# Background transfers of a Strassen stage: pinned in program order, handed out one at a time, with fewer steps

## The chip, the cores and the metric

The kernel runs on one core of a Trainium2 chip. The metric is the device time of one execution in microseconds; lower is better. The core has five engines with a queue each: PE (TensorE, the matrix engine), DVE (VectorE), ACT (ScalarE), POOL (GpSimd) and SP (SyncE, which only issues transfers). Each engine takes its queue in order. DMA transfers are issued from SP, ACT and POOL; only POOL's can add to what they write.

## The reference

One layer of a hybrid decoder trunk: the input (16 prepended meta tokens and 1024 tokens of 1024 channels) is normalised, projected, and read by three causal mixers: gated DeltaNet (`dn`, 8 heads), short gated convolution (`sc`) and Mamba-2 SSD (`sd`). Their outputs meet in a gated sum and an output projection:

```python
xn = rms_norm(x, norm_pre)
proj = xn @ w_in                      # every mixer's inputs, and the gate logits
ys = stack([y_ssd, y_sc, y_dn])
branch = einsum("btnw,nwd->btnd", ys, w_branch)
gates = sigmoid(gate_logits)          # (tokens, 3, 1024)
merged = sum(gates * branch, axis=2)
return x + rms_norm(merged @ w_out, norm_post)
```

All in float32, with seven 1024x1024x1024 products in the last part: three for the gates, three for the branches, one for the output.

## The kernel before

The kernel has two parts. The first (up to about 1325 us) projects the stream and runs the mixers: eight heads of `dn` (`dn_mix`), then eight tiles of `sd` (`sd_mix`). These are long chains of small operations on PE, DVE, ACT and POOL; `weave` fills PE between them with the dense projections of the next head or of `sc`. A mixer is a generator: at each `yield` the program takes some dense matmuls. The weights of a dense job are loaded by SP (L148), cast by ACT (L156) and their rest taken by DVE (L157), one job ahead.

The second part is the Strassen stage. Each of the seven products is a group of seven half-size products, 49 steps in all, and a step is four quarters (`q`) of 12 matmuls of 128x512: 48 matmuls. For each operand on the right (`x`, `dn`, `sc`, `sd`, `wo`) there are seven blocks of 1 MB in HBM: the quarters `11` and `22`, the negated `n21`, and the sums `t1` to `t4`. The program computes the sums by transfers alone: `sums` copies a block on POOL's queue and adds a second to it (an accumulating transfer), eight transfers for one operand:

```python
for dst, a, b in (("t1", "n12", "11"), ("t2", "t1", "22"),
                  ("t3", "n12", "22"), ("t4", "t2", "n21")):
    GP.dma_start(o[dst], o[a])
    GP.dma_start(o[dst], o[b], accum_op=ALU.add, max_dma_last_dim=2048)
```

During step n, `t_load` asks on SP for the two pieces (`tr`, 512 KB each) of step n+2; `t_prep` casts those of step n+1 (ACT `th`, DVE `tl`), `w_prep` its weights (ACT and DVE `w`), `left_sum` forms the sums on the left (DVE), `finish` takes the results off. Left blocks (`a11`, `a12`, `a21`, `a22`, 1 MB each; `a__...` in the trace) of the next group are loaded at steps 3 to 6 of a group, those of the first group at the stage's start. The first two steps take their right operand from the stream in SBUF (`xh`, `xl`).

Four kinds of background work make the operands. `right_x` (in head 0) stores the stream's quarters, the negated ones by way of ACT and a tile of the pool tag `t` (five buffers, shared with the mixers' rows and raw convolution inputs), the second half `xl` by accumulating transfers; then `sums("x")`. `right_wo` (in head 2) does it for `w_out`. `beside` takes one piece of such work at every third yield. `sc` stores its blocks on SP and starts `sums("sc")` after its last tile; `sums("dn")` runs beside `sd` tile 1. For `sd` the rows must be scaled by a norm that is known only after the last tile: `scale_tasks` (in steps 2 to 8 of the stage, one task at each quarter) loads a 1 MB block of `y_sd` as four pieces, multiplies it on DVE by the broadcast `rins`, stores it from ACT, and after four blocks starts `sums("sd")`.

Three things set the order. The program's text gives each instruction a rank. A scheduler then orders each engine's queue by simulated time: it takes the first in rank among those whose inputs it takes as landed, so that an instruction with nothing to wait for may come out far ahead of its place. And the chip takes each queue in that order, whatever lands when. `tc.keep_in_program_order` ties an instruction behind the one before it in the program on its engine.

Lines that the change and the steps of the prediction touch: `sums` L119 to L127, stores of `dn` L732, `sc` L765, `y_sd` L884, `rin_d` L904; `right_x` L906 (ACT L922, L924, POOL L913, L926); `right_wo` L930 (L936, L938, L941); `left blocks` L1047, `t_load` L1093, `t_prep` L1103 and L1104, `w_prep` L1112 to L1120, `left_sum` L1126, `out_setup` L1190 (`gpost`, asked for at step 42), `scale_tasks` L1221 to L1248 (`ys` L1234, L1239, L1243). In `dn_mix`, L636 is a memset on POOL that the delta solve needs at each level.

## Time and profile before

| | us |
|---|---|
| median of 3 runs (lowest, highest) | 1901.55 (1897.69, 1906.21) |
| profiled execution | 1900.59 |
| its span in the trace | 1898.3 |

| engine | busy us | share of the span |
|---|---|---|
| PE | 1824.3 | 96% |
| DVE | 1263.6 | 67% |
| ACT | 839.5 | 44% |
| POOL | 189.7 | 10% |

The trace moves 225.76 MB by DMA. The span is from the first to the last instruction that the profiler saw. PEclk is the clock that TensorE was granted, as a share of its full speed (1.00 is 2.4 GHz, 0.50 is 1.2 GHz). In the chain of waits each piece is what the next one waited for, followed back from the end. A wait for several things is put down to the one that came last. Transfers are named by what they write and read (`out<-in`), with the line and queue that issued them.

### The profile page before, as it was taken

The page shows a single profiled execution, that of the slowest core. Times are in us where ns is not written, and L with a number is a line of the kernel's source. Part 1 is how long each engine was busy: PE and PEld are TensorE (multiplying, and loading weights), DVE is VectorE, ACT ScalarE, POOL GpSimd, SP SyncE. Part 2 cuts the span into 40 slices and gives each one's busy share as a digit, 9 for nine tenths or more (in the row PEclk, how much of TensorE's full clock was granted, in tenths as well). Part 3 has the DMA queues.
Part 4 walks back from the last instruction along what each step waited for, and adds up shares of the span by engine and source line. Part 5 has one row for each costly group of instructions (what it writes and reads, how often), then busy time and mean ns, then how long its engine had stood idle before and what let it go on. Part 6 is the DMA issues. An engine that isn't in the chain of part 4 may idle for free.

```text
span 1898.3 us, 27585 instructions
## 1 busy us (share of the span) xinstructions
PE 1824.3 (96%) x11115; PEld 1578.8 (83%) x11115; DVE 1263.6 (67%) x1866; ACT 839.5 (44%) x1353; POOL 189.7 (10%) x335
## 2 busy tenths in 40 slices
PE   3998999999999999999999999999889999999997
PEld 3896989888998989888889899887668888888886
DVE  4554675656656656575756887786566857867687
ACT  4452534425243342434434556452335455455444
POOL 2021101101011110101001111110000000000000
PEclk8999999999999999999999999999889999999999
DMA  6568113821117221111123423221999443544532
GB/s 194 115 163 192 56 46 123 227 62 40 50 46 209 70 61 40 45 56 46 34 79 88 126 89 96 62 87 34 326 327 280 155 161 128 177 150 139 178 109 91
DMA packets 153258, 225.76 MB, mean 119 GB/s; under 512 B 11009, under 2 KB 97214, under 8 KB 152298
## 3 DMA queue, kind: packets, MB, share of 16 engines
q1 hardware_dynamic: 135162, 162.65, 27.1%
q0 software_dynamic: 12976, 46.66, 10.6%
q10 hardware_dynamic: 4992, 14.68, 2.0%
q8 instruction: 87, 1.43, 0.3%
q14 instruction: 41, 0.34, 0.1%
HBM read 192.41 MB, written 75.61 MB: 141 GB/s over the span
## 4 chain that ended last, share of the span: by engine, by line
PE 82%; DMA 7%; DVE 6%; issue 2%; ACT 1%; SPq 0%; POOL 0%; DVEq 0%; ACTq 0%; POOLq 0%
PE py L1141 5%; PE py L1140 5%; PE py L1139 5%; PE pz L1141 3%; PE pz L1140 3%; PE pz L1139 3%; DMA a__13462<-in_w_in_dram 1%; DMA ys<-y_sd 1%; DMA a__13776<-in_w_branch_dram 1%; DVE w L157 1%; DMA won<-in_w_out_dram 1%; DVE gt L1217 1%; DMA wo<-in_w_out_dram 1%; DMA xt<-in_x_dram 0%; DMA x_n<-xn 0%
## 5 line engine op out<-in xcount | busy, mean ns | idle before, releaser
L1141 PE MATMUL py<-th,w 128*128 128x512 f32 x432 | 170.1, 394 | 5.7 <-DVE w L1117 5.7
L1139 PE MATMUL py<-th,w 128*128 128x512 f32 x432 | 169.7, 393 | 1.7 <-ACT u L1151 1.7
L1140 PE MATMUL py<-tl,w 128*128 128x512 f32 x432 | 169.5, 392 | 1.9 <-DVE tl L1104 1.9
L1104 DVE TENSOR_TENSOR tl<-tr,th 128x1024 fp32r<-128x1024 f32 x94 | 114.1, 1222 | 67.4 <-ACT th L1103 66.8
L1103 ACT CAST th<-tr 128x1024 fp32r<-128x1024 f32 x94 | 98.4, 1052 | 106.0 <-PE py L1141 52.6
L1139 PE MATMUL pz<-th,w 128*128 128x512 f32 x320 | 124.5, 389 | 0.0
L1140 PE MATMUL pz<-tl,w 128*128 128x512 f32 x320 | 124.5, 389 | 0.0
L1141 PE MATMUL pz<-th,w 128*128 128x512 f32 x320 | 124.5, 389 | 0.0
L157 DVE TENSOR_TENSOR w<-raw,w 128x1024 fp32r<-128x1024 f32 x84 | 103.5, 1232 | 10.5 <-ACT w L156 9.8
L1141 PEld LDWEIGHTS py<-th,w 128*128 128x128 f32 x432 | 82.1, 190 | 23.5 <-DVE w L1117 6.5
L1140 PEld LDWEIGHTS py<-tl,w 128*128 128x128 f32 x432 | 82.0, 190 | 19.5 <-DVE tl L1104 2.3
L156 ACT CAST w<-raw 128x1024 fp32r<-128x1024 f32 x84 | 88.0, 1048 | 23.1 <-PE sc2h L180 4.0
L1139 PEld LDWEIGHTS py<-th,w 128*128 128x128 f32 x432 | 82.1, 190 | 19.2 <-ACT u L1151 2.1
L1140 PEld LDWEIGHTS pz<-tl,w 128*128 128x128 f32 x320 | 60.1, 188 | 12.5
L1139 PEld LDWEIGHTS pz<-th,w 128*128 128x128 f32 x320 | 60.1, 188 | 12.4
L1141 PEld LDWEIGHTS pz<-th,w 128*128 128x128 f32 x320 | 60.1, 188 | 12.4
L1151 ACT COPY u<-py 128x1024 f32<-128x1024 f32 x30 | 30.4, 1013 | 43.6 <-PE py L1141 38.3
L1164 DVE TENSOR_TENSOR u<-pz,u 128x1024 f32<-128x1024 f32 x30 | 36.6, 1219 | 7.6 <-PE pz L1141 7.6
L239 PE MATMUL xp<-ident,xg 128*128 128x128 f32 (+1 forms) x72 | 11.0, 304 | 21.2 <-DVE xg L233 20.8
L1170 ACT ACTIVATE gt<-u 128x1024 f32<-128x1024 f32 x14 | 14.8, 1061 | 31.7 <-DVE u L1164 31.5
L239 PEld LDWEIGHTS xp<-ident,xg 128*128 128x128 f32 (+1 forms) x72 | 9.4, 162 | 22.4 <-issue 20.9
L470 ACT ACT_TABLE_LOAD x18 | 23.1, 1283 | 4.5 <-PE sd3z L180 1.1
(1878 smaller groups left out, 5622.2 us busy)
## 6 DMA issues: line engine op xcount, KB each, us to landing
raw<-in_w_in_dram SPq DMA_DIRECT2D x84, 512.0 KB, 3.9
tr<-x_t SPq DMA_DIRECT2D x24, 512.0 KB, 4.1
tr<-x SPq DMA_DIRECT2D x10, 512.0 KB
ys<-y_sd SPq DMA_DIRECT2D x16, 256.0 KB, 10.2
tr<-dn_t SPq DMA_DIRECT2D x8, 512.0 KB, 6.0
tr<-sc_t SPq DMA_DIRECT2D x8, 512.0 KB, 3.7
tr<-sd_t SPq DMA_DIRECT2D x8, 512.0 KB, 3.5
tr<-wo_t SPq DMA_DIRECT2D x8, 512.0 KB, 3.6
```

The source lines that it names most:

```text
L156: A.copy(wh, raws[i])
L157: V.tensor_tensor(wl, raws[i], wh.bitcast(F32), ALU.subtract)
L239: PE.transpose(pv[:, k, :], xg[:n, kk * P:(kk + 1) * P], ident[:n, :n])
L470: lambda o, c0, n: A.activation(dst[:, c0 - META:c0 - META + n], o, fn), name=name)
L1103: A.copy(h, src)
L1104: V.tensor_tensor(l, src, h.bitcast(F32), SUB)
L1139: PE.matmul(o, lhsT=w[:, 0, k, cs], rhs=r1, start=fresh and k == 0, stop=False, skip_group_check=not fresh)
L1140: PE.matmul(o, lhsT=w[:, 0, k, cs], rhs=r2, start=False, stop=False, skip_group_check=not fresh)
L1141: PE.matmul(o, lhsT=w[:, 1, k, cs], rhs=r1, start=False, stop=k == HK - 1, skip_group_check=not fresh)
L1151: A.copy(t, g.ps["y", u])
L1164: V.tensor_tensor(k, t, k, ADD)
L1217: V.scalar_tensor_tensor(o, o, tot, fin["x", t][:, es], ALU.mult, ADD)
```

## The change

- Blocks `n12` are gone. `quarters` names for each quarter the blocks it is stored into: a negated upper right quarter goes straight into `t1` and `t3`, and `sums` adds `11` and `22` to them. `t2` and `t4` are made as before. Six transfers per operand are left.
- `background` pins a transfer in program order on its queue. `sums` and all transfers of `right_x` and `right_wo` use it.
- `right_x` adds or negates the pair `xh`, `xl` on DVE in one instruction per half quarter, and stores the result from ACT. The diagonal blocks of `w_out` are no longer copied: sums and the stage read them from `w_out` (`wo_straight`).
- `beside` takes a piece at every ninth yield and does not drain the rest; `early` (x, then w_out) runs beside all eight heads, `late` (sums of `dn`) beside the `sd` tiles.
- The stores of `sc`, `y_sd` and `rin_d` are issued by ACT instead of SP.
- `scale_tasks` works on eight pieces of 512 KB, with two buffers (tag `gpost`) and one row buffer of its own, one half piece per step from step 5 to 20 (`q` = 2).
- `sums("sc")` is taken at steps 3, 5, ... 13 and `sums("sd")` at steps 23, 25, ... 33, each piece behind a copy of one column (`tick`) on POOL that reads the step's `th`.

```diff
@@ -111,19 +111,25 @@
...
     OPS = ("11", "n21", "t2", "t3", "t1", "t4", "22")
-    opd = {s: {o: dram.tile([P, HK, HALF], F32, name=f"{s}_{o}") for o in OPS + ("n12",)}
+    opd = {s: {o: dram.tile([P, HK, HALF], F32, name=f"{s}_{o}") for o in OPS}
            for s in ("x", "dn", "sc", "sd", "wo")}
-    def quarter(s, i, j):
-        return opd[s][("" if i == j else "n") + f"{i + 1}{j + 1}"]
-    def sums(s):
-        o = opd[s]
-        for dst, a, b in (("t1", "n12", "11"), ("t2", "t1", "22"), ("t3", "n12", "22"), ("t4", "t2", "n21")):
-            GP.dma_start(o[dst], o[a])
-            yield 0
-            GP.dma_start(o[dst], o[b], accum_op=ALU.add, max_dma_last_dim=2048)
+    def quarters(s, i, j):
+        return [opd[s][n] for n in {(0, 0): ("11",), (0, 1): ("t1", "t3"), (1, 0): ("n21",), (1, 1): ("22",)}[i, j]]
+    def background(eng, *args, **kw):
+        tc.keep_in_program_order(eng.dma_start(*args, **kw))
+    def sums(s, straight=None):
+        o = dict(opd[s], **(straight or {}))
+        for dst, a, b in (("t1", None, "11"), ("t3", None, "22"), ("t2", "t1", "22"), ("t4", "t2", "n21")):
+            if a:
+                background(GP, o[dst], o[a])
+                yield 0
+            background(GP, o[dst], o[b], accum_op=ALU.add, max_dma_last_dim=2048)
             yield 0
@@ -729,7 +735,8 @@
...
         for j in range(2):
-            DMA.dma_start(quarter("dn", h // HK, j)[:, h % HK, :], zT[:, j * HALF:(j + 1) * HALF])
+            for dst in quarters("dn", h // HK, j):
+                DMA.dma_start(dst[:, h % HK, :], zT[:, j * HALF:(j + 1) * HALF])
@@ -762,12 +769,10 @@
...
                 V.scalar_tensor_tensor(s, o, 1.0 if t // HK == j else -1.0, s, ALU.mult, ALU.mult)
-                DMA.dma_start(quarter("sc", t // HK, j)[:, t % HK, :], s)
+                for dst in quarters("sc", t // HK, j):
+                    A.dma_start(dst[:, t % HK, :], s)
             yield from dense(w, xh, xl, TWO, use, name=n + "b")
-            if t == KT - 1:
-                for _ in sums("sc"):
-                    pass
@@ -881,7 +886,7 @@
...
             yield 600
-        DMA.dma_start(y_sd[t], zT)
+        A.dma_start(y_sd[t], zT)
         for b in BIG:
@@ -901,31 +906,28 @@
...
                 V.reciprocal(sqa[b][0:1, :], sqa[b][0:1, :])
-                DMA.dma_start(rin_d[t // 4][:, b.outs], sqa[b][0:1, :])
+                A.dma_start(rin_d[t // 4][:, b.outs], sqa[b][0:1, :])
...
-        o = opd["x"]
         for i in range(2):
-            ks, ts = slice(i * HK, (i + 1) * HK), slice(META + i * HALF, META + (i + 1) * HALF)
-            dst = quarter("x", i, i)
-            A.dma_start(dst, xh[:, ks, ts].bitcast(F32))
-            GP.dma_start(dst, xl[:, ks, ts].bitcast(F32), accum_op=ALU.add)
-        yield 0
-        for i in range(2):
-            ts = slice(META + (1 - i) * HALF, META + (2 - i) * HALF)
-            for u in range(2):
-                ks = slice(i * HK + 2 * u, i * HK + 2 * u + 2)
-                dst = quarter("x", i, 1 - i)[:, 2 * u:2 * u + 2, :]
-                for part in (xh, xl):
-                    t = tmp(f"xn{i}{u}")[:, :SEQ].rearrange("p (k t) -> p k t", k=2)
-                    A.mul(t, part[:, ks, ts].bitcast(F32), -1.0)
-                    if part is xh:
-                        A.dma_start(dst, t)
+            for j in range(2):
+                ts = slice(META + j * HALF, META + (j + 1) * HALF)
+                for u in range(2):
+                    ks = slice(i * HK + 2 * u, i * HK + 2 * u + 2)
+                    t = tmp(f"xr{i}{j}{u}")[:, :SEQ].rearrange("p (k t) -> p k t", k=2)
+                    h, l = xh[:, ks, ts].bitcast(F32), xl[:, ks, ts].bitcast(F32)
+                    if i == j:
+                        V.tensor_tensor(t, h, l, ALU.add)
                     else:
-                        GP.dma_start(dst, t, accum_op=ALU.add)
+                        V.scalar_tensor_tensor(t, h, -1.0, l, ALU.mult, ALU.subtract)
+                    for dst in quarters("x", i, j):
+                        background(A, dst[:, 2 * u:2 * u + 2, :], t)
                     yield 0
...
+    wo_straight = {n: w_out[i * HALF:(i + 1) * HALF, i * HALF:(i + 1) * HALF].rearrange("(k p) f -> p k f", p=P)
+                   for i, n in enumerate(("11", "22"))}
@@ -933,15 +935,13 @@
...
                 t = tmp(f"won{i}{u}")[:, :SEQ].rearrange("p (k t) -> p k t", k=2)
-                DMA.dma_start(t, rows.rearrange("(k p) f -> p k f", p=P))
+                background(DMA, t, rows.rearrange("(k p) f -> p k f", p=P))
                 yield 0
                 A.mul(t, t, -1.0)
-                A.dma_start(quarter("wo", i, 1 - i)[:, 2 * u:2 * u + 2, :], t)
+                for dst in quarters("wo", i, 1 - i):
+                    background(A, dst[:, 2 * u:2 * u + 2, :], t)
                 yield 0
-            A.dma_start(quarter("wo", i, i), w_out[i * HALF:(i + 1) * HALF, i * HALF:(i + 1) * HALF].rearrange(
-                "(k p) f -> p k f", p=P))
-            yield 0
-        yield from sums("wo")
+        yield from sums("wo", wo_straight)
@@ -965,31 +965,26 @@
...
-    def beside(main, side, every=3):
-        side = side()
+    def beside(main, side, every):
...
             yield want
-            if n % every == 0:
+            if n % every == every - 1:
                 next(side, None)
-        for _ in side:
-            pass
+    early = (lambda: (yield from chain(right_x, right_wo)))()
+    late = sums("dn")
...
             lambda: sdg_jobs(0, grps[0]), lambda: sd_jobs(0, sdt[0])]
-        mix = lambda h=h: dn_mix(h, dnt[h])
-        if h in (0, 2):
-            mix = lambda mix=mix, side=(right_x, right_wo)[h // 2]: beside(mix, side)
-        slot(4 + n, mix, lambda n=n: sc_next(n), *fs)
+        slot(4 + n, lambda h=h: beside(lambda: dn_mix(h, dnt[h]), early, 9), lambda n=n: sc_next(n), *fs)
     for t in range(KT):
...
             lambda t=t, g=g: sd_mix(t, grps[g], sdt[t])]
-        mix = lambda gens=gens: chain(*gens)
-        if t == 1:
-            mix = lambda mix=mix: beside(mix, lambda: sums("dn"))
+        mix = lambda gens=gens: beside(lambda: chain(*gens), late, 9)
         fs = []
@@ -1056,7 +1051,9 @@
...
             self.wsrc = {"g": cols_of(w_in, C_G + b * D), "b": cols_of(w_branch[b])}.get(kind)
-            self.ops = opd["x" if kind == "g" else "wo" if kind == "o" else ("sd", "sc", "dn")[b]]
+            self.ops = opd["x" if kind == "g" else ("sd", "sc", "dn")[b]]
+            if kind == "o":
+                self.ops = dict(opd["wo"], **wo_straight)
@@ -1186,7 +1183,7 @@
...
     def out_setup():
-        fin["gpost"] = c1.tile([P, D], F32, name="gpost", tag="gpost")
+        fin["gpost"] = c1.tile([P, D], F32, name="gpost", tag="gpost", bufs=2)
         DMA.dma_start(fin["gpost"], norm_post.broadcast_to([P, D]))
@@ -1219,35 +1216,36 @@
     def scale_tasks():
-        box = {}
-        def rins():
-            box["r"] = c2[0].tile([P, HK, HALF], F32, name="rins", tag="mg01")
-            for i in range(2):
-                DMA.dma_start(box["r"][:, 2 * i:2 * i + 2, :], rin_d[i].broadcast_to([P, SEQ]).rearrange(
-                    "p (j t) -> p j t", j=2))
-        def one(i, j, tag):
-            def load():
-                box[i, j] = c2[0].tile([P, HK, HALF], F32, name=f"ys{i}{j}", tag=tag)
-                for k in range(HK):
-                    DMA.dma_start(box[i, j][:, k, :], y_sd[i * HK + k][:, j * HALF:(j + 1) * HALF])
-            def mul(k):
-                t = box[i, j][:, k, :]
-                n = i * HK + k
-                V.scalar_tensor_tensor(t, t, (snw if i == j else nsnw)[:, n:n + 1], box["r"][:, 2 * i + j, :],
-                                       ALU.mult, ALU.mult)
-            def store():
-                A.dma_start(quarter("sd", i, j), box[i, j])
-            return [load] + [lambda k=k: mul(k) for k in range(HK)] + [store]
-        per = [one(0, 0, "mg00"), one(0, 1, "mg10"), one(1, 0, "mg11"), one(1, 1, "mg00")]
-        return [rins] + [f for p in per for f in p] + [lambda: [None for _ in sums("sd")]]
-    extra = scale_tasks()
+        for i in range(2):
+            for j in range(2):
+                js = slice(j * HALF, (j + 1) * HALF)
+                r = c1.tile([P, HALF], F32, name=f"rin{i}{j}", tag="rin")
+                DMA.dma_start(r, rin_d[i][:, js].broadcast_to([P, HALF]))
+                for u in range(2):
+                    t = c1.tile([P, 2, HALF], F32, name=f"ys{i}{j}{u}", tag="gpost", bufs=2)
+                    n = i * HK + 2 * u
+                    for k in range(2):
+                        DMA.dma_start(t[:, k, :], y_sd[n + k][:, js])
+                    yield 0
+                    for k in range(2):
+                        w = (snw if i == j else nsnw)[:, n + k:n + k + 1]
+                        V.scalar_tensor_tensor(t[:, k, :], t[:, k, :], w, r, ALU.mult, ALU.mult)
+                    for dst in quarters("sd", i, j):
+                        A.dma_start(dst[:, 2 * u:2 * u + 2, :], t)
+                    yield 0
+    scale, sd_sums, sc_sums = scale_tasks(), sums("sd"), sums("sc")
+    tick = c1.tile([P, 1], F32, name="tick", tag="tick")
+    def extra(n, q):
+        if q == 2 and 5 <= n < 21:
+            next(scale, None)
+        side = sc_sums if n in range(3, 15, 2) else sd_sums if n in range(23, 35, 2) else None
+        if q == 3 and side is not None:
+            h = groups[n // 7].t[n % 7, 0][0]
+            tc.keep_in_program_order(GP.tensor_copy(tick, h[:, 0, 0:1].bitcast(F32)))
+            next(side, None)
@@ -1298,8 +1296,7 @@
...
                     finish(g, 1, 0, u)
-            if (0, 2) <= (g.n, ph) and extra:
-                extra.pop(0)()
+            extra(n, q)
             product(g, ph, q)
```

## Rows read from the trace of the kernel before

**Rows 1.** The page's first part: busy us (share of the span) xinstructions.
```profile
PE 1824.3 (96%) x11115; PEld 1578.8 (83%) x11115; DVE 1263.6 (67%) x1866; ACT 839.5 (44%) x1353; POOL 189.7 (10%) x335
```

**Rows 2.** The windows view: window and length, engines' busy us, PEclk, DMA share, GB/s.
```profile
100.00:200.00 100.00, 93.62 (x679) 81.36 (x678) 55.89 (x108) 43.69 (x87) 21.14 (x37) 0.98 0.70 174
...
1300.00:1400.00 100.00, 84.96 (x349) 67.19 (x347) 56.54 (x54) 36.41 (x39) 4.64 (x6) 0.93 0.77 249
1400.00:1450.00 50.00, 44.61 (x178) 36.29 (x179) 38.23 (x35) 23.39 (x24) 4.15 (x5) 0.90 1.04 319
...
1600.00:1700.00 100.00, 100.00 (x443) 82.84 (x442) 74.20 (x65) 48.07 (x48) 0.00 (x0) 1.00 0.46 150
...
1330.00:1335.00 5.00, 2.07 (x4) 1.26 (x5) 2.13 (x2) 1.99 (x2) 0.67 (x1) 0.50 1.06 336
...
1355.00:1360.00 5.00, 4.34 (x13) 3.47 (x14) 5.00 (x5) 4.19 (x5) 0.00 (x0) 0.66 1.03 324
...
1400.00:1405.00 5.00, 3.55 (x8) 2.81 (x9) 1.39 (x2) 0.00 (x0) 1.04 (x1) 0.50 0.94 396
```

**Rows 3.** The waits of PE: waiting line <- releaser: us in total, times, longest.
```profile
PE sm L353 <- ACT xh L241: 9.4, 2, 9.1
PE py L1139 <- ACT w L1119: 8.5, 1, 8.5
PE py L1141 <- DVE w L1117: 5.7, 2, 3.9
PE dm0u L648 <- POOL dm0Z L636: 4.6, 2, 3.6
PE pz L1141 <- DVE w L1120: 2.6, 1, 2.6
PE dm2z L616 <- DVE dm2C L609: 2.5, 2, 1.5
```

**Rows 4.** The chain of waits, 0 to 62 us: start us, us, what.
```profile
0.81 10.28 DMA wo<-in_w_out_dram
...
34.15 9.36 DMA xt<-in_x_dram
```

**Rows 5.** The chain of waits, 100 to 205 us.
```profile
168.40 5.57 DMA x_t<-x_t
```

**Rows 6.** The chain of waits, 340 to 380 us.
```profile
355.60 11.27 DMA won<-in_w_out_dram
```

**Rows 7.** SP's queue at the stage's start: start us, us, line, what.
```profile
1325.10 0.34 SPq L765 DMA_DIRECT2D sc<-sc7a  x1
1325.54 0.38 SPq L1047 DMA_DIRECT2D a__13450<-in_w_in_dram  x1
...
1340.01 2.26 SPq L1190 DMA_DIRECT2D gpost<-in_norm_post_dram  x1
```

**Rows 8.** The waits of SP's queue, whole span.
```profile
SPq L765 <- DVE sc7a L764: 10.8, 2, 5.6
```

**Rows 9.** The waits of ACT and DVE, 1310 to 1460 us.
```profile
ACT w L1119 <- DMA a__13450<-in_w_in_dram: 18.0, 1, 18.0
DVE ys L1239 <- DMA ys<-y_sd: 13.4, 5, 4.7
```

**Rows 10.** The page's costliest groups: busy us, mean ns of one, idle before.
```profile
L1164 DVE TENSOR_TENSOR u<-pz,u 128x1024 f32<-128x1024 f32 x30 | 36.6, 1219 | 7.6 <-PE pz L1141 7.6
```

**Rows 11.** The DMA view: transfer, queue, xcount, KB each, median us to landing.
```profile
ys<-y_sd SPq DMA_DIRECT2D x16, 256.0 KB, 10.2
...
x_t<-x POOLq DMA_DIRECT2D x3, 1024.0 KB, 11.8
...
sc_t<-sc POOLq DMA_DIRECT2D x3, 1024.0 KB, 13.7
...
a__13462<-in_w_in_dram SPq DMA_DIRECT2D x1, 1024.0 KB, 23.9
...
a__14757<-in_w_branch_dram SPq DMA_DIRECT2D x1, 1024.0 KB, 4.7
...
x_t<-x_t POOLq DMA_DIRECT2D x2, 7.3
```

## Prediction

> **What bounds the kernel now.** I read the page's first part first: TensorE (PE) is busy 96% of the span [rows 1], so time can come only from its idle 74 us and from stretches at the lower clock. The windows view says where these are [rows 2]: 1600 to 1700 us stands for the whole later half of the Strassen stage (443 matmuls in 100.00 us, clock 1.00), so nothing is to be had there. 100 to 200 leaves PE 6.38 us idle, 1300 to 1400 15.04 us and 1400 to 1450 5.39 us. The clock in the last two is 0.93 and 0.90, that is at most 7 + 5 = 12 us of full-speed clocks given away, part of them while PE idled anyway. So the passage from the mixers into the Strassen stage costs 20.4 us of idle time and some 8 to 12 of half clock, about 29. The rest of the 74 us lies mostly in the first 60 us and after the last matmul.
>
> The waits of PE [rows 3] name the causes: 8.5 us for the first weight block of the stage (ACT's cast), 2.6 and 5.7 us for DVE's `w`; 4.6 us in `dm0u` for a POOL memset (`dm0Z`), 2.5 us in `dm2z`. The chain of waits then shows that behind four of these stands background traffic. At the very start it is `wo<-in_w_out`, 10.28 us, though the program asks for it only in head 2 [rows 4]. In head 0 the chain goes through `x_t<-x_t`: POOL stood in its queue before a copy whose source had not landed, and the memset that PE needed stood behind it [rows 5]. In head 2 it is `won<-in_w_out`, 11.27 us [rows 6]. At the passage SP held the first block's load back behind the last `sc` store: `sc<-sc7a` leaves at 1325.10, `a__13450` at 1325.54 [rows 7], after SP had waited 10.8 us for `sc7a` [rows 8]. ACT then waits 18.0 us for that block, and DVE 13.4 us for `ys` [rows 9].
>
> **The change part by part.** A Strassen step is 48 matmuls, by the 443 in 100 us 10.8 us; I use it below as a unit.
>
> *Negated blocks straight into two sums.* For each of five operands the `n12` block and its two copies into `t1` and `t3` (1 MB each, on POOL's queue) go; the block is stored twice instead. `sums` falls from 8 POOL transfers to 6. For `x` the six accumulations of `xl` go too, since DVE adds or negates the pair in SBUF: 8 instructions of 128x1024 at 1219 ns, the nearest row of that shape [rows 10], are 9.8 us of DVE in place of 8 multiplications on ACT. They lie beside dense matmuls in heads 0 to 2, where DVE is busy 55.9 of 100 us [rows 2]; uncovered they would cost up to 9.8.
>
> *Pinned and handed out every ninth yield.* The floating goes: no transfer can leave before its place in the program on its queue. That removes three things. (a) The two 1 MB `wo` loads at 0.81 us vanish altogether, since the Strassen stage reads the diagonal of `w_out` itself. The chain gives them 10.28 us [rows 4], but three small loads of many pieces stand behind them and would have taken part of that time themselves, and PE's 9.4 us wait at 45 us hangs on `xt`, which goes out only at 34.15 after SP waited for DVE. Bounds 0 and 7; nearest is less than half of 10.28, so I take 3. (b) In head 0 the two PE stalls go: 6.4 us idle, about 1 of half clock. Bounds 0 (POOL still waits, for other transfers) and 7.4. Nine yields are about 15 us (head 0 has some 60 yields and fills the 100 us of its window), longer than the 7.3 to 11.8 us that such transfers of `x` take to land [rows 11], so POOL should find each source landed: I take 6. Next late there would be the delta chain itself. (c) In head 2 the wait for `won`: the load is pinned, ACT's multiplication behind it is not, so the same wait can come back; bounds -2 (four such loads, all four stalling at 1.1 us each) and 2.5, I take 1.
>
> *Stores moved from SP to ACT* (20 for `sc`, 8 `y_sd`, 4 `rin_d`). The price is ACT waiting in order for DVE's product, with weight casts and the exponentials of the mixers behind it. No row shows this for `sc`; SP's own two waits for `sc7a` were 10.8 us [rows 8], but SP had nothing else to do and stood there early, while ACT comes there later. Bounds -11 (32 issues of 0.34 us [rows 7], none covered) and 0; ACT is busy 43.69 of 100 us in the mixers [rows 2], nearer to the second, so I take -2. The gain is the head of the stage: SP no longer stands before `sc7a`, so `a__13450` can leave as soon as its memory is free. If that is 6 us or more before the last `sc` matmul, PE's 8.5 us and the half clock after them (about 2.7: the granted clock is 0.50 in 1330 to 1335 [rows 2], and it takes some 5 us of work at that rate until it is back) go, 11.2 in all; if the memory is itself freed by `sc7a`, nothing goes. I take 9, the rest being cast and subtraction.
>
> The Trainium skill, DMA: Bandwidth & Descriptors, section "Issuing engines are not separate DMA queues", speaks against this part: transfers started from different engines end on the same 16 DMA engines, and spreading them saves only the sequencer's issue time. Issue time is what the 0.34 us of the `sc7a` store is; by that rule the nine would be under one, and the forecast about 1884. The rows that decide are the wait and the order of issue, 10.8 us in one queue [rows 7, 8]: it is a queue standing still, not a lack of engines.
>
> *`sc` sums out of the passage* (from 1328 us to steps 3 to 13, one transfer every second step). While they ran, `a__13462` needed 23.9 us to land; the same form later in the stage needs 4.7 [rows 11]. PE's 2.6 us with some 1.7 of half clock (0.66 over the 5 us of 1355 to 1360 [rows 2]) hang on it. Bounds 0 and 4.3; three blocks and four pieces of `x_t`, 5 MB, still come at once, so I take 3.
>
> *Rows scaled piecewise, `sd` sums at steps 23 to 33.* What is left of the passage, 1375 to 1420, is 20.4 - 8.5 - 2.6 = 9.3 us of idle time and about 4 of half clock (0.50 again in 1400 to 1405 [rows 2]), 13.3: DVE stands before `ys` [rows 9], and PE before DVE's `w` (5.7 us, [rows 3]). Two loads of 256 KB per piece instead of eight, and the sums 170 us later, should remove most. But pieces are not pinned. The row of `gpost` shows what the scheduler does with such loads: the program asks for it at step 42, and it left at 1340.01, in step 0 [rows 7]. So the pieces will start long before step 5, as fast as two buffers let them. Bounds -10 (the case below at a quarter of its price) and 13; I take 6. DVE's 16 multiplications are as many as before. The `tick` makes POOL wait for a step's cast, with only the next sum behind it; its sources have two steps, 21.6 us, against 13.7 us to land [rows 11].
>
> Sum: 3 + 6 + 1 - 2 + 9 + 3 + 6 = 26 us. The profiled execution took 1900.59 us (span 1898.3 and 2.3 around it), 1.0 under the median of the runs shown. 1900.6 - 26 = 1874.6, against the median 1875.5.
>
> **The rivals.** *The pieces are not handed out at all.* They crowd at the passage as the loads did before, and the change does there not what it says: of the 18 us at the passage some 5 stay, and 5 + 8 elsewhere give 1888. For it: `gpost` in step 0 [rows 7]. Against: the `sc` and `sd` sums are pinned, which takes about half of the passage's traffic away.
>
> *All of it goes*: 7 + 7.4 + 2.5 at the mixers and 28 at the passage, 45 us, 1857. For it: the whole later stage runs at 100% with the same prefetch [rows 2]. Against: 5 MB at once at its start.
>
> *Slower: DVE stands in order before each piece.* The scheduler believes a piece landed, sets its multiplication between the subtractions of a step, and the chip lands it late. `ys` takes 10.2 us to land [rows 11]; DVE is busy 74.2 of 100 us in the stage [rows 2], so two steps have 5.6 us to spare. A wait of the whole landing for each of 8 pieces costs 8 x (10.2 - 5.6) = 37, less the 26: 1912. It decides from 5.6 + 26/8, about 8.9 us per piece. For it: DVE's 13.4 us before `ys`, longest 4.7 [rows 9]. Against: those were five waits under eight loads at once.
>
> **How the numbers follow.** Forecast 0.50 (1875, its own range 1863 to 1887), pieces crowding 0.22 (1888), all of it 0.18 (1857), slower 0.10 (1912). About 0.5% (9.5 us) is what a measurement of this kernel can tell from no change. Faster by more: nearly all of the forecast, all of the third and three fifths of the second case, 0.80. Within it: 0.11. Slower: 0.09. The range 1858 to 1897 leaves out the slower case and the last of the best.
>
> **What would show it.** Right: no `wo` load at the start; in head 0 no wait of PE on `dm0Z`; the first stage matmul within 3 us of the last `sc7b` one, `a__` blocks landing in under 12 us; POOL's sums one by one, two steps apart. Wrong: DVE waits for `ys` over 30 us in sum, ACT waiting for DVE before its stores with PE idle behind it, or the first block's load still leaving at the end of `sc7a`.

## The result and the profile after

The changed kernel takes 1873.71 us (median of 4 runs, 1870.37 to 1876.62), the kernel before 1901.16 (1897.69 to 1906.21): ratio 0.9853, 95% interval [0.9824, 0.9882], 27.5 us faster. The forecast was 1875 us. The total is right; its terms are not, and large misses of opposite sign cancel, so that the sum came out is luck. Below, "before" and "after" name the two kernels.

The profiled execution took 1870.37 us (span 1868.6). The 29.7 us between the spans, split at the first matmul of a mixer's transposes (`dm0pk`, `dm1pk`, ...) and at the end of the last projection product (`sc7b`; at the last start of the first of its three lines), behind which the Strassen stage begins:

| stretch | before | after | gain | forecast |
|---|---|---|---|---|
| start to head 0 (`dm0pk`) | 103.1 | 86.6 | 16.5 | 3 |
| head 0 | 128.3 | 121.0 | 7.3 | 6 |
| head 1 | 107.7 | 114.9 | -7.2 | 0 |
| head 2 | 122.3 | 118.8 | 3.5 | 1 |
| head 3 to the last `sc7b` | 862.1 | 862.1 | 0.0 | -2 |
| stage | 574.8 | 565.2 | 9.6 | 18 |

These are single traces; the same start in another trace ends up to 3 us away (85.8 to 89.6 in the runs below that leave it as it is).

PE is busy 98% of the span now [rows 1]; the page's first part of after:

```profile
PE 1822.4 (98%) x11115; PEld 1576.0 (84%) x11115; DVE 1271.7 (68%) x1874; ACT 829.5 (44%) x1343; POOL 200.1 (11%) x331
```

*Start.* The windows view (columns as in [rows 2]) of the first 50 us, first before, then after:

```profile
0.00:50.00 50.00, 19.97 (x104) 17.19 (x105) 23.00 (x48) 22.80 (x47) 11.62 (x54) 0.84 0.60 190
...
40.00:50.00 10.00, 4.73 (x16) 3.58 (x17) 4.52 (x10) 4.74 (x11) 0.00 (x0) 0.50 0.34 134
```

```profile
0.00:50.00 50.00, 34.80 (x205) 29.90 (x205) 28.48 (x59) 28.32 (x59) 14.16 (x55) 1.00 0.49 144
```

Twice as many matmuls (205 for 104) stand in the same 50 us. The kernel before idled at 40 to 50 us and had 0.50 of the clock there. SP's queue in after (start us, us, line, what):

```profile
16.93 4.03 SPq L154 DMA_DIRECT2D raw<-in_w_in_dram  x2
...
22.87 3.90 SPq L226 DMA_DIRECT2D xt<-in_x_dram  x3
```

The last three blocks of the input leave at 22.87, where before they left at 34.15 [rows 4].

*Head 1*, new in after. Waits of PE (columns as in [rows 3]; the one in head 1 is that of `dm1ms`, the others are of the stage), and POOL's queue:

```profile
PE py L1138 <- DVE w L1117: 4.6, 2, 4.0
PE dm1ms L731 <- ACT dm1oh L722: 3.2, 1, 3.2
PE py L1136 <- ACT w L1113: 2.7, 1, 2.7
PE py L1136 <- ACT w L1116: 2.3, 1, 2.3
```

```profile
257.11 1.08 POOL L123 DMA_DIRECT2D x_t<-x  x1 [0.23 <-issue]
...
296.64 1.28 POOL L724 TENSOR_TENSOR dm1ol<-dm1osq,dm1oh 128x512 fp32r<-128x512 f32 x1 [0.73 <-ACT dm1oh L722]
297.87 1.04 POOL L123 DMA_DIRECT2D x_t<-x  x1
306.24 0.53 POOL L123 DMA_DIRECT2D x_t<-x_t  x1 [7.33 <-DMA x_t<-x]
312.36 1.04 POOL L123 DMA_DIRECT2D x_t<-x_n  x1 [5.59 <-DMA x_t<-x_t]
313.03 1.65 POOL L720 TENSOR_TENSOR dm1osq<-dm1osq,dn1q 128x512 f32<-128x512 f32 x1
```

The first sum of `x` leaves at 257.11, well inside head 1 (207.6 to 322.5); before, all of them ran in head 0, from 130.2 to 174.5. The last three came out back to back between the two halves of head 1's output norm. POOL waited 7.33 and 5.59 us for their sources while `dm1osq`, which PE's `dm1ms` needs, stood behind them. PE loses 4.0 us idle between 305 and 325 us, and has 0.66 of its clock in the second half of that.

*Stage.* Windows of 50 us from each kernel's own stage start, first before, then after:

```profile
1323.50:1373.50 50.00, 38.84 (x150) 30.34 (x149) 24.89 (x22) 18.19 (x19) 3.61 (x4) 0.86 0.99 301
1373.50:1423.50 50.00, 40.72 (x159) 32.16 (x158) 31.05 (x34) 16.72 (x18) 2.57 (x4) 0.90 0.98 332
1423.50:1473.50 50.00, 50.00 (x223) 41.40 (x222) 34.61 (x30) 28.30 (x30) 3.62 (x4) 1.00 0.90 266
```

```profile
1303.40:1353.40 50.00, 45.73 (x197) 36.52 (x196) 32.76 (x32) 22.37 (x23) 1.49 (x2) 1.00 0.81 263
1353.40:1403.40 50.00, 42.77 (x171) 33.02 (x169) 29.18 (x29) 18.34 (x20) 2.90 (x4) 0.93 0.92 299
1403.40:1453.40 50.00, 48.63 (x205) 39.57 (x206) 36.15 (x33) 27.36 (x28) 3.36 (x4) 0.97 0.72 232
```

Counting matmuls is the shortest reading: at full rate a window holds 222.5, 667 in the three. Before did 532 of them, after 573; the 41 more are 9.2 us at 0.225 us each, nearly the whole gain of the stage. The first window alone gained 47 (10.6 us); the second and third together lost 6 (1.4 us). All later windows are full in both until the tail. Still 94 (21 us) are missing in after. The first two lines below are waits of DVE and ACT in it, the others its DMA view (columns as in [rows 9, 11]):

```profile
DVE ys L1232 <- DMA ys<-y_sd: 23.0, 6, 7.4
ACT u L1148 <- DVE ys L1232: 8.9, 1, 8.9
```

```profile
ys<-y_sd SPq DMA_DIRECT2D x16, 256.0 KB, 5.8
...
a__13450<-in_w_in_dram SPq DMA_DIRECT2D x1, 1024.0 KB, 11.0
```

The fourth left block now lands in 11.0 us instead of 23.9 [rows 11], but DVE stands 23.0 us before `ys`, more than the 13.4 of before [rows 9]. DVE's queue shows the pieces far from steps 5 to 20, which would be about 1360 to 1530:

```profile
1336.54 0.73 DVE L1232 SCALAR_TENSOR_TENSOR ys<-ys,snw,rin 128x512 f32<-128x512 f32 x1
...
1349.42 0.75 DVE L1232 SCALAR_TENSOR_TENSOR ys<-ys,nsnw,rin 128x512 f32<-128x512 f32 x1 [5.02 <-DMA ys<-y_sd]
...
1399.90 0.75 DVE L1232 SCALAR_TENSOR_TENSOR ys<-ys,snw,rin 128x512 f32<-128x512 f32 x1 [7.42 <-DMA ys<-y_sd]
...
1406.27 1.41 DVE L1232 SCALAR_TENSOR_TENSOR ys<-ys,snw,rin 128x512 f32<-128x512 f32 x2
```

### The profile page after: what moved, and what is told of

Its sections match the earlier page's. It is cut to its first block, busy times and chain, and to the rows that moved or that the text cites. A ratio compares the mean times of both kernels' runs of the same rounds, so it can differ in the third digit from the quotient of the medians.

```text
span 1868.6 us, 27595 instructions
## 1 busy us (share of the span) xinstructions
PE 1822.4 (98%) x11115; PEld 1576.0 (84%) x11115; DVE 1271.7 (68%) x1874; ACT 829.5 (44%) x1343; POOL 200.1 (11%) x331
## 4 chain that ended last, share of the span: by engine, by line
PE 85%; DVE 5%; DMA 5%; ACT 2%; issue 2%; POOL 1%; SPq 0%; DVEq 0%; ACTq 0%; POOLq 0%
PE py L1136 4%; PE py L1138 4%; PE py L1137 4%; PE pz L1138 3%; PE pz L1136 3%; PE pz L1137 3%; DMA ys<-y_sd 1%; DMA a__13748<-in_w_branch_dram 1%; DMA a__13450<-in_w_in_dram 1%; DVE gt L1214 1%; DMA sd_t<-ys 0%; DMA gain<-in_norm_pre_dram 0%; DMA sd_n<-ys 0%; DVE tl L1101 0%; DVE w L163 0%
## 5 line engine op out<-in xcount | busy, mean ns | idle before, releaser
L1138 PEld LDWEIGHTS pz<-th,w 128*128 128x128 f32 x320 | 60.1, 188 | 15.4 <-DVE w L1114 1.9
L1247 POOL COPY tick<-th 128x1 f32<-128x1 f32 x12 | 16.3, 1358 | 377.8 <-ACT th L1100 377.8
L1167 ACT ACTIVATE gt<-u 128x1024 f32<-128x1024 f32 x14 | 14.9, 1061 | 26.9 <-DVE u L1161 26.7
L245 PE MATMUL xp<-ident,xg 128*128 128x128 f32 (+1 forms) x72 | 11.8, 319 | 12.2 <-DVE xg L239 10.7
```

The lines of the kernel that those rows point to most:

```text
L1138: PE.matmul(o, lhsT=w[:, 1, k, cs], rhs=r1, start=False, stop=k == HK - 1, skip_group_check=not fresh)
L1247: tc.keep_in_program_order(GP.tensor_copy(tick, h[:, 0, 0:1].bitcast(F32)))
```

## The experiments

Edits are to the changed kernel unless said otherwise. Ratios are to the kernel before, run in the same group. Its median was 1901.16 us beside after, 1904.13 beside e1, e2, e3 and e7, 1898.74 beside e4, e5, e6 and e8, and 1904.59 beside e9 to e12; so times of different groups compare to a few us only, and the ratios compare better. "Stage" is the stretch of the table above. A trace is of one execution, which lies up to 4.9 us from its kernel's median (after 3.3 below, e3 4.9 below, e9 4.2 above).

**What made the start faster.** e1 brings the two 1 MB loads of `w_out`'s diagonal back, unpinned, into blocks that nothing reads.

```diff
+        for n, q in wo_straight.items():
+            A.dma_start(opd["wo"][n], q)
         yield from sums("wo", wo_straight)
```

> The changed kernel, with the two 1 MB loads of w_out's diagonal issued again from ACT, unpinned, into blocks that nobody reads. Theory A (these two loads are what the start lost: they take bandwidth and hold the next loads back): the transposes of head 0 begin at 100 to 103 us as before the change, not at 86.6, and the time is 1885 to 1890 us. Rival (the start gained because the stream's stores at 48 and 59 us are gone, or because SP's order of loads came out otherwise by itself): head 0 begins within 3 us of 86.6, time 1873 to 1877.

Measured: 1889.64 us, 0.9929 [0.9905, 0.9953]; head 0 begins at 101.5. The start's gain is lost, nearly all of it. SP's queue of e1:

```profile
26.96 7.13 SPq L154 DMA_DIRECT2D raw<-in_w_in_dram  x2
34.20 4.73 SPq L226 DMA_DIRECT2D xt<-in_x_dram  x3
```

It is the order of before again: `xt` leaves 11.3 us later than in after. The first projection matmul is 6.0 us late (25.3 for 19.3), head 0 14.9. So in this trace the smaller part has arisen by the first projection; the other 8.9 us arise behind it, where `xt` leaves late and the clock is 0.53 in 40 to 50 us.

e9 loads the same blocks, but as pinned background pieces.

```diff
+        for n, q in wo_straight.items():
+            background(A, opd["wo"][n], q)
+            yield 0
         yield from sums("wo", wo_straight)
```

> The changed kernel, with the two 1 MB copies of w_out's diagonal back, this time pinned at their place in right_wo (heads 3 and 4). Theory A (the copies cost 15 us by the moment at which they ran, not by their bytes): head 0 begins within 2 us of 86.6, time 1870 to 1876 us. Rival (the bytes cost wherever they run): 1880 or more.

Measured: 1875.75 us, 0.9846 [0.9809, 0.9882]; head 0 at 89.5, 1 us outside of what was expected, but e11 below, with the mixers of after, has 89.6. The two loads leave at 528 and 541 us here and cost nothing that shows. The place of these loads costs the 15 us, not their bytes.

e10 is the kernel before with this one part of the change: `wo_straight` in place of the two loads.

```diff
-            A.dma_start(quarter("wo", i, i), w_out[...])
-            yield 0
-        yield from sums("wo")
+        yield from sums("wo", wo_straight)
```

> The kernel before, with one part of the change alone: the diagonal of w_out is read from w_out itself, in the sums and in the stage, and its two copies are gone. Theory A (most of the change's gain in the first 100 us is this part): head 0 begins at 86 to 90 us instead of 103.1, time 14 to 17 us under the kernel before, about 1885 to 1888. Rival (the stores of x that still float to 48 and 59 us hold the start): head 0 begins at 95 or later, under 9 us gained.

Measured: 1898.02 us, 0.9968 [0.9951, 0.9986]. The first projection matmul is at 19.3 us as in after, yet head 0 begins at 101.1, 2.0 earlier than before, as the rival has it. The median is 6.6 us under that of the kernel before beside it; where more than those 2.0 come from, the traces do not show. The chain of waits of e10 and its windows:

```profile
34.73 11.15 DMA x<-xh
49.71 7.16 DMA rows<-in_dn_norm_dram
```

```profile
50.00:60.00 10.00, 3.28 (x13) 3.03 (x12) 0.73 (x4) 1.51 (x2) 0.16 (x1) 0.74 1.06 193
60.00:80.00 20.00, 20.00 (x100) 18.94 (x99) 13.62 (x25) 9.40 (x13) 0.00 (x0) 0.79 0.10 26
```

With the `wo` loads gone, the unpinned stores of `x` float into the start, and a small load of rows behind them takes 7.16 us; PE idles 6.7 us in 50 to 60 us, with the chain through that load, and works on at a lower clock. The rest of the change without the end of these loads is worth 1.6 us at head 0 (e1), the end of the loads alone 2.0 (e10), both together 16.5. That the second cause is the stores of `x` is read from the chain of e10; no run takes them away alone. It is not their pin: in e7 below, without pins, no store of `x` leaves in the first 85 us, and DVE makes the first block for them at 94.8.

**What the `sc` stores on ACT are worth.** e2 puts them back on SP.

```diff
-                    A.dma_start(dst[:, t % HK, :], s)
+                    DMA.dma_start(dst[:, t % HK, :], s)
```

> The changed kernel, with the stores of sc issued by SP again. Theory A (SP's queue standing before the last store held the first weight block of the Strassen stage): PE waits 7 to 9 us for it again, with half clock after it, time 1882 to 1886 us. Rival by the page's rule that the issuing engine makes no difference but the issue time: under 1 us, 1873 to 1875. Rival (the wait comes back but later stalls shrink by as much): PE waits 7 to 9 us at the stage's start and the time is 1874 to 1878.

Measured: 1877.49 us, 0.9866 [0.9845, 0.9886]; stage 570.9, 5.7 longer. PE's wait of before is back, as in theory A, and the time is that of the last rival. The wait, the stage's first window, and SP's queue:

```profile
PE py L1136 <- ACT w L1116: 9.5, 1, 9.5
```

```profile
1304.50:1354.50 50.00, 40.44 (x165) 32.13 (x164) 28.95 (x27) 21.99 (x22) 1.37 (x2) 0.90 0.80 257
```

```profile
1306.12 0.34 SPq L773 DMA_DIRECT2D sc<-sc7a  x1
1306.63 0.38 SPq L1042 DMA_DIRECT2D a__13438<-in_w_in_dram  x1
```

In after that block left far earlier:

```profile
1293.16 0.37 SPq L1042 DMA_DIRECT2D a__13438<-in_w_in_dram  x1
```

That is 14.3 us before the next of SP's blocks, and PE waits 2.3 us. In e2 SP had waited 45.2 us, in two waits, for DVE's `sc7a` before its last two `sc` stores. The first window has 165 matmuls for 197, 7.2 us less; the next two have 385 for 376, so part of it is won back. How much reaches the end is not clear of noise: 3.8 us by the medians, 2.5 by the ratios, whose intervals overlap. By the Trainium skill, DMA: Bandwidth & Descriptors, section "Issuing engines are not separate DMA queues", a move between issuing engines saves the sequencer's time alone, 0.34 us here. This trace does not agree: SP's queue, standing before the store, also held the block behind it, and PE's wait grew from 2.3 to 9.5 us.

**What the handed-out `sc` sums are worth.** e3 issues them after the last `sc` tile, unpinned, as before (`sums_now` is the six transfers).

```diff
+            if t == KT - 1:
+                sums_now("sc")
-        side = sc_sums if n in range(3, 15, 2) else sd_sums if ...
+        side = sd_sums if n in range(23, 35, 2) else None
```

> The changed kernel, with the six transfers of the sc sums asked for right after the last sc tile, unpinned, as before the change. Theory A (they compete with the first blocks of the stage): the fourth block takes 18 to 24 us to land instead of 11, PE stalls for it, time 1878 to 1884 us. Rival (the first blocks are limited by their own 5 MB): under 2 us, 1873 to 1876.

Measured: 1879.79 us, 0.9874 [0.9847, 0.9900], by the ratio 4 us more than after, with intervals that overlap; stage 572.4, 7.2 longer. The DMA view, a wait and the stage's first window:

```profile
a__13456<-in_w_in_dram SPq DMA_DIRECT2D x1, 1024.0 KB, 20.4
```

```profile
PE pz L1148 <- DVE w L1127: 5.1, 1, 5.1
```

```profile
1300.80:1350.80 50.00, 39.03 (x151) 30.18 (x150) 27.70 (x27) 18.11 (x18) 3.60 (x4) 0.91 0.94 274
```

The fourth left block (named 13456 here) takes 20.4 us for 11.0, as theory A has it. The first window has 151 matmuls for 197, 10.4 us less; the next two have 391 for 376.

**What the pins are worth in all.** e7 keeps every part of the change, its spacing too, without `keep_in_program_order`.

```diff
-        tc.keep_in_program_order(eng.dma_start(*args, **kw))
+        eng.dma_start(*args, **kw)
-            tc.keep_in_program_order(GP.tensor_copy(tick, ...))
+            GP.tensor_copy(tick, ...)
```

> The changed kernel without any pin in program order: the same transfers, asked for at the same places, free to float. Theory A (the pins carry the gain): sums leave as soon as the scheduler takes their sources as landed, so POOL's queue stalls the solve in head 0 by 5 to 8 us again and sd sums crowd steps 4 to 12; time 1883 to 1895 us. Rival (fewer transfers, and no copies of w_out, carry it): 1870 to 1877.

Measured: 1895.80 us, 0.9952 [0.9935, 0.9970], 0.8 above theory A's range. Head 0 is 4.5 us longer (POOL waits 12.0 us for `x_t<-x` there, with `dm0osq` behind it), head 2 7.4, the stage 13.9; head 1 is 6.8 shorter, since no sum stands before `dm1osq` there. The start stays fast (87.8).

**What the pieces cost.** e4 pins all of the row scaling: loads and stores (one of the loads is shown) and multiplications.

```diff
-                DMA.dma_start(r, rin_d[i]...)
+                background(DMA, r, rin_d[i]...)
-                        V.scalar_tensor_tensor(t[:, k, :], ...)
+                        tc.keep_in_program_order(V.scalar_tensor_tensor(t[:, k, :], ...))
```

> The changed kernel, with the loads, multiplications and stores of the row scaling pinned in program order too, so that they stand at steps 5 to 20. Theory A (in the changed kernel they float to steps 2 to 8 and stand before DVE's work there, 23.0 us of DVE waits): DVE waits for ys under 6 us in sum, PE idles under 5 us between 1310 and 1450 instead of 12, time 1861 to 1866 us. Rival (the passage is limited by its loads, and DVE would wait for blocks instead): time 1871 to 1876. Rival (pinned multiplications stall later steps): over 1876.

Measured: 1856.29 us, 0.9766 [0.9742, 0.9791], better than any theory; stage 549.5, 15.7 shorter. PE does not idle between 1310 and 1450 us, where it idles 10.05 us in after (the expectation says 12). Its windows from the stage's start:

```profile
1302.00:1352.00 50.00, 47.20 (x199) 37.98 (x198) 31.59 (x28) 25.29 (x26) 2.13 (x3) 0.97 0.70 223
1352.00:1402.00 50.00, 50.00 (x222) 41.40 (x221) 39.57 (x37) 27.65 (x28) 5.43 (x6) 1.00 0.76 239
1402.00:1452.00 50.00, 50.00 (x223) 41.40 (x222) 35.35 (x33) 23.28 (x23) 3.31 (x4) 1.00 0.93 284
```

644 of 667 matmuls: the stage is full from its second window on, with 239 and 284 GB/s beside it in the second and third.

e11 pins the multiplications alone; loads and stores float as in after.

```diff
-                        V.scalar_tensor_tensor(t[:, k, :], ...)
+                        tc.keep_in_program_order(V.scalar_tensor_tensor(t[:, k, :], ...))
```

> The changed kernel, with only DVE's multiplications of the row scaling pinned in program order; loads and stores of the pieces may float. Theory A (the cost is DVE standing in order before a piece that has not landed): nearly all of what pinning everything gave, DVE waits for ys under 3 us, time 1855 to 1862 us. Rival (the cost is the loads of the pieces crowding the stage's own loads): under half of it, 1866 to 1873.

Measured: 1857.59 us, 0.9752 [0.9722, 0.9782]; stage 549.8, that of e4. No wait of DVE for `ys` is left. DVE's and SP's queues:

```profile
1381.34 1.41 DVE L1233 SCALAR_TENSOR_TENSOR ys<-ys,snw,rin 128x512 f32<-128x512 f32 x2
1404.01 1.41 DVE L1233 SCALAR_TENSOR_TENSOR ys<-ys,snw,rin 128x512 f32<-128x512 f32 x2
```

```profile
1328.36 0.37 SPq L1228 DMA_DIRECT2D ys<-y_sd  x1
1332.85 1.42 SPq L1228 DMA_DIRECT2D ys<-y_sd  x3
1389.00 0.79 SPq L1228 DMA_DIRECT2D ys<-y_sd  x2
```

The first four loads still leave at 1328 to 1333, about as early as in after, and cost nothing that shows. Two buffers hold the later ones back until a multiplication in its place has freed one. So what cost the 15.7 us was, by the 23.0 us of DVE's waits that are gone, DVE standing in its queue before data that was not there. One share stays open: the pin also spreads the other twelve loads, which leave at 1389 to 1497 here and by 1400 in after, and a load lands in 3.9 us in the median here for 5.8. All sixteen loads early with DVE held in place was not tried.

**The stall in head 1.** e5 ties each background transfer on POOL behind the last 40 POOL instructions of the program, not the last one alone.

```diff
+        if eng is GP:
+            for i in before[-40:-1]:
+                tc.add_manual_dep(ins.ins, i.name, ...NoSync...)
```

> The changed kernel, with each background transfer of POOL tied behind the last 40 POOL instructions before it in the program, not only the last one. Theory A (the last one had itself floated, so three sums of x stood before POOL's part of head 1's end and PE idled 4.0 us, with half clock after it): head 2 begins at 315 to 317 us instead of 322.5, time 1866 to 1868 us. Rival (the sums then wait and stall another head): 1872 to 1876.

Measured: 1868.39 us, 0.9832 [0.9807, 0.9857]. POOL's queue in e5:

```profile
298.62 1.04 POOL L123 DMA_DIRECT2D x_t<-x  x1
308.49 1.29 POOL L725 TENSOR_TENSOR dm1osq<-dm1osq,dn1q 128x512 f32<-128x512 f32 x1 [8.82 <-ACT dm1osq L724]
...
311.73 0.55 POOL L123 DMA_DIRECT2D x_t<-x_t  x1
```

The second sum now stands behind `dm1osq`, which runs 4.5 us earlier; head 2 begins at 316.1 for 322.5. In this trace only 1.2 of these 6.4 us are left at the end, as the stage, whose pieces still float, came out 4.7 longer (554 matmuls in its first 150 us). The median is 5.3 us lower and the ratio 4 us, with intervals that overlap; e6 against e4, where no piece floats, is the cleaner pair.

e6 is e4 and e5 together.

> Both edits at once: the row scaling pinned and POOL's transfers tied behind 40 instructions. Theory A (two separate stalls): the gains add, 15 to 20 us under the changed kernel, 1854 to 1859 us. Rival (one of them was no stall on the path): 1862 to 1868.

Measured: 1849.67 us, 0.9731 [0.9707, 0.9755], below the expected 1854. It is 6.6 us under e4 of the same group, with no run in common (the highest of e6 is 1850.25, the lowest of e4 1853.30); head 1 is 107.8 long for 113.6 in e4, the stages are alike (549.9 and 549.5). Two waits of PE are left in the stage:

```profile
PE py L1141 <- ACT w L1121: 2.3, 1, 2.3
...
PE py L1143 <- DVE w L1122: 0.5, 1, 0.5
```

**Whether six transfers are better than eight.** e8 stores the negated block once, into `n12`, and lets POOL copy it; the eight sums are pinned and handed out.

```diff
-   (0, 1): ("t1", "t3")
+   (0, 1): ("n12",)
-   ("t1", None, "11"), ("t3", None, "22")
+   ("t1", "n12", "11"), ("t3", "n12", "22")
-   range(3, 15, 2), range(23, 35, 2)
+   range(3, 19, 2), range(21, 37, 2)
```

> The changed kernel, with each negated block stored once and copied into both sums by POOL's transfers again, eight per operand, but pinned and handed out as in the change. Theory A (what counts is when they run, not how many): 1872 to 1877 us. Rival (ten more copies of 1 MB stall POOL's queue in the heads or the loads of the stage): 1880 to 1890.

Measured: 1865.52 us, 0.9819 [0.9791, 0.9847], faster than either theory. Head 1 is 107.8 long for 114.9: with two more pieces at the front, others fall into it, and `dm1osq` runs at 307.95. The stage is 5.1 shorter, with 8.3 us of DVE's waits for `ys`. That neither is a merit of eight transfers, and only what is not held in place fell elsewhere, is what e12 tests.

e12 is e6 with the blocks of e8, where all of it is held.

> The fastest form so far (row scaling pinned, POOL's transfers tied behind 40 instructions), with the negated blocks stored once and copied into both sums by POOL again, eight transfers per operand instead of six. Theory A (the number of background transfers costs nothing as long as none stands before PE's work; the gain of the copies in the changed kernel was only that the stall of head 1 fell away): within 3 us of 1849.7. Rival (the doubled stores on ACT cost time by themselves): 1842 to 1846.

Measured: 1849.35 us, 0.9710 [0.9678, 0.9741]; stage 549.6 for 549.9. The intervals of e6 and e12 overlap. Two transfers per operand, the part of the change that leaves out most work, bring nothing measurable (the ratios differ by 0.0021, some 4 us, in favour of eight). These two are the fastest versions, 23 and 27 us under the changed kernel by the ratios.

## Why the prediction was right in sum and wrong in its terms

*The start* (forecast 3, measured 16.5) is the term that failed most. The step: the 10.28 us of the `wo` loads were taken as transfer time that others share, "less than half", and PE's 9.4 us wait for `xt` was left standing because SP sends it only after DVE. That order itself hung on the `wo` loads: `xt` leaves at 22.79 in e10 without them, at 34.20 in e1 with them. The floating `x` stores were not priced for the start at all, though e10 shows them there. Two causes stood one behind the other, and the change took both.

*Head 0* (6, measured 7.3) held as a number: there is no `dm0Z` wait of PE, and e7, without pins, loses 4.5 of it. But not in the way forecast. The sums of `x` were to run in head 0 with each source landed; they left head 0 altogether. Eight pieces of stores at every ninth yield take 72 yields, more than the some 60 of a head by the prediction's own count, so the sums come in head 1. There they are 5 to 31 us apart, not 15, and POOL waits 3.95, 7.33 and 5.59 us for their sources. What head 0 gained, head 1 lost.

*Head 1* (0, measured -7.2) was not foreseen. The other step behind it: "no transfer can leave before its place in the program on its queue". The pin ties a transfer only to the POOL instruction just before it in the program, and that one may float ahead itself. Tied behind 40 instructions (e5, e6), the sums leave PE alone, and head 1 is 107.7 and 107.8 long, as before.

*Head 2* (1, measured 3.5): 1.0 above its upper bound of 2.5. The wait that was left open did not come back: in after PE waits for nothing in head 2, before it waited 2.5 us for `dm2C`.

*Stores on ACT* (-2, measured about 0): from head 3 to the last `sc7b` after takes 862.1 us, and e2, with the `sc` stores on SP, 862.3. One trace of the price stays at the stage's head: ACT issues the last `sc` store at 1305.03 after 11.8 us of waiting for DVE, and the first weight cast at 1305.48 behind it; PE's 2.3 us there may come from this, which was not tried.

*First block* (9) and *`sc` sums* (3). Together they came out nearly as forecast: the stage's first window gained 47 matmuls, 10.6 us, for 12. How the gain is shared can't be had by subtraction: put back alone, the one takes 32 of the 47 (e2, 7.2 us), the other 46 (e3, 10.4 us), so the two cover each other in part. The mechanism of the first was right: the first stage matmul starts at 1306.58, 2.3 us after the end of the last `sc7b` (1304.28). The `sc` sums were priced too low: the bound of 4.3 counted PE's one wait in the trace of before and not that the same traffic delays what follows.

*Pieces* (6; measured -1.4, the six matmuls fewer in the second and third window). This step failed, and in the way that the first and the last rival describe. The pieces were not handed out, as "pieces are not pinned" said; and DVE stood in order before them, 23.0 us in sum with 7.4 the longest, below the 8.9 per piece at which it would have turned the whole slower. The 6, chosen between -10 and 13, goes by fewer loads at once and later sums; which engine's queue the consumer stands in was left to the last rival, at 0.10. e4 and e11 put the price of the unpinned pieces at 15.7 and 15.4 us.

In sum: 13.5 us too few at the start, 3.8 too few in heads 0 and 2, 2 too few for the stores, against 7.2 in head 1 and 8.4 in the stage too many: 3.7 us of gain more than the forecast of 26. "All of it goes", 1857, was nearest to what the design can give; e11 reached it by one more pin (1857.59), e6 went below it.

What stays open: why stages with unpinned pieces differ by up to 10 us (565.2 in after, 569.9 in e5 and e9, 560.1 in e8 with its two more sums per operand). In after, e5 and e9 DVE takes the pieces in the same order, and what differs is how soon their loads land (5.8, 6.7 and 9.8 us in the median); in e8 the order differs. What decides the one or the other was not tried.

## What to carry to other kernels

An instruction that waits for a slow transfer must be held in place in the in-order queue where it waits: pinning the consumer alone (e11) was worth 15 us, while the four loads that still left early cost nothing that shows. A pin to the neighbour in program order is only as good as the neighbour; tie background work behind the instructions that the critical engine needs (e5). Before pricing a stall at the length of one wait, look for the second cause behind it: at the start neither of two causes moved head 0 by more than 2.0 us alone, and both moved it by 16.5; in the stage two waits covered each other, so that what either costs alone does not add up.

## What was not expected of the hardware

- Two loads of 1 MB at 0.81 us cost 15 us of the end time (e1), where one such block lands in 4.7 us later in the trace [rows 11]: late inputs left PE idle, and the granted clock fell to 0.50 to 0.53 in 40 to 50 us.
- The copy of one column on POOL (`tick`, L1247) takes 1.24 us in the median of 12 (0.19 to 5.30), about as long as a pass over two tiles of 128x512 there (`dm1ol` above, 1.28 us).
- The landing time of a 1 MB block at the same place in the program was 23.9 us in before, 11.0 in after and 20.4 in e3, by whether the `sc` sums ran beside it.
